# Two-operand GpSimd instructions of a hybrid decoder step: from whole tiles to pieces of at most 256 elements

## Chip, core and metric

The kernel runs on one core of a Trainium2 chip. The metric is the device time of one execution in microseconds (us); lower is better. Engines are named as the profile names them: PE (TensorE), DVE (VectorE), ACT (ScalarE), POOL (GpSimd), SP (SyncE, which issues the DMAs).

## The reference

One decoder layer over a prompt of 2048 tokens of 1024 features and 8 decoding sequences of 4 tokens, all in float32:

```python
h = rmsnorm(x, g_mix)
proj = h @ w_in                         # u | q | k | v | g
ssm_out = s5_mixer(u, ...)              # diagonal complex state space, scan over tokens, GELU, GLU
ret_out = retention_mixer(q, k, v, g)   # 4 heads, rope on q and k, chunks of 128, group norm, gate
x = x + concat([ssm_out, ret_out]) @ w_out
x = x + memory_attend(rmsnorm(x, g_xattn), mk, mv, w_mq, w_mo)   # 4 heads, 256 memory tokens
h = rmsnorm(x, g_mlp)
x = x + square(relu(h @ w_up)) @ w_down
y = rmsnorm(x, g_final)
```

The new states of the scan and the retention and the memory's keys and values are outputs too.

## The kernel before

Every matmul of float32 operands is made of three passes: an operand is split into a high part, rounded by ACT to the matmul's number format, and a low part, the operand minus its high part, by DVE or POOL. Activations lie with features in the partitions and tokens along the row, in four blocks of 512 tokens; the second block also carries the 32 sample tokens, so its tiles are 544 wide. Weights come in units of 128 x 1024 (`raw`), are split into `whl` and used at once.

The work has two large parts. The **mixer** (the first 990 us) goes through the four blocks: projection to v, then for each of four heads q, k and g (`head_items`), then u. Beside the projections run side chains: the retention of a head (`retention`: transposes `pkd`, products `psc`, `pkv`, `po`, a group norm on DVE, transpose `pt`), and the scan of the block before (`s5_batch`, four batches a block: matmuls `vr`, `vi`, DVE and POOL turn and scan them, matmul `py`, transpose `pf`). The memory's keys and values and the fold of the query and output weights follow, with the last block's scan beside them. The **rest** (990 us to the end) takes each block through attention (`sc`, softmax, `ptp`), the MLP (`up_items`, `down_items`) and the output projection of the next block.

The order on all engines is written at build time by a recording layer. `Engine.__getattr__` (line 189) wraps every call of an engine: it tells a planner (`Model.done`) what is written and read and then issues the instruction. The planner holds a time at which each engine comes free; it charges POOL 140 ns for an instruction and 2.11 ns an element, DVE 65 ns and 1.042 ns. PE's main stream of projections polls side chains whose planned wake time has come (`Order.poll`), so a planned duration sets after which matmul a chain's next matmul stands. Work with the key `E("...")` goes to DVE or POOL by a table (`SET`: 0 DVE, 1 POOL, 2 the one that the planner has done sooner); the weights' low part may be left open in the same way. Each engine then works through its own queue strictly in that order.

POOL makes: the low parts of some weight units, in four instructions of 256 elements each (`split_unit`, `lo`); and, in one instruction each, the second half of rope (`kr` and `qr`, 512 or 272 wide), four to six steps of each scan batch (`t`, `gl`, `Yi`; 512 or 4 x 129 = 516 elements), the sums of squares for the norms (`acc`), the low part of the MLP's activation (`actl`, 512 or 544), the tables of the scan at the start, and some smaller things. All calls go through line 197, so the trace has one line for them and is read by tile names.

Of the kernel before, what the change touches and what calls it, by code (L numbers as in the profile page):

```python
# [10 lines left out]
F32 = mybir.dt.float32  # L11
# [3 lines left out]
ALU = mybir.AluOpType  # L15
# [167 lines left out]
class Engine:  # L183
# [5 lines left out]
    def __getattr__(self, name):  # L189
        f = getattr(self.eng, name)  # L190

        def call(*args, **kw):
            outs = [x for x in ([kw["out"]] if "out" in kw else list(args[:1])) + [kw.get("accum_out")] if x is not None]
            ins = [x for x in list(args[0 if "out" in kw else 1:]) + [v for k, v in kw.items() if k not in ("out", "accum_out")]
                   if isinstance(x, bass.AP)]
            self.model.done(self.key, name, outs, ins, args[2] if name == "activation" else None)
            return f(*args, **kw)  # L197
        return call


class Either:
# [127 lines left out]
def tile_decoder_step(ctx: ExitStack, tc: tile.TileContext, ins: dict, outs: dict):  # L329
    nc = tc.nc  # L330
    model = Model()
    V, A, G, SY = (Engine(model, e, k) for e, k in ((nc.vector, "V"), (nc.scalar, "A"), (nc.gpsimd, "G"), (nc.sync, "SP")))
# [90 lines left out]
    def split_unit(raw, eng, pool=None, tag="whl", bufs=NW):  # L423

        hl = (pool or wpool).tile([P, 2, 1024], F32R, tag=tag, name=tag, bufs=bufs)
        A.activation(hl[:, 0, :], raw, AF.Copy)

        def lo():
            e = eng or min((V, G), key=lambda e: max(model.free[e.key], model.ready(hl)) + 1024 * Model.RATE[e.key][1])
            n = 256 if e is G else 1024  # L430
            for i in range(0, 1024, n):
                e.tensor_tensor(out=hl[:, 1, i:i + n], in0=raw[:, i:i + n], in1=hl[:, 0, i:i + n].bitcast(F32), op=ALU.subtract)
        return hl, lo

    od = Order(model, load_unit, split_unit)
# [46 lines left out]
    def pieces(t):  # L482
        return [(0, t)] if t <= 512 else [(0, t // 2), (t // 2, t // 2)]
# [1891 lines left out]
```

## Time and profile before

| What | Value |
|---|---|
| median of three runs | 3056.98 us (3055.93 to 3063.95) |
| profiled execution, device time | 3057.99 us |
| its span | 3055.8 us, 2.2 us less than its device time |
| PE busy | 2944.5 us, 96% of the span |
| DVE, ACT, POOL busy | 1767.3 us (58%), 1007.1 us (33%), 1314.5 us (43%) |
| instructions on POOL | 1463 |

The page's table of slices shows PE at eight or nine tenths in most slices of the first third and at nine tenths or more nearly everywhere later; DVE is at seven to nine tenths in the first quarter of the span and at three to five tenths later. A busy POOL or DVE instruction in the records includes the time in which it has begun and waits for a port.

### The profile page before, as it was taken

The page shows a single profiled execution, that of the slowest core. Times are in us where ns is not written, and L with a number is a line of the kernel's source. Part 1 is how long each engine was busy: PE and PEld are TensorE (multiplying, and loading weights), DVE is VectorE, ACT ScalarE, POOL GpSimd, SP SyncE. Part 2 cuts the span into 40 slices and gives each one's busy share as a digit, 9 for nine tenths or more (in the row PEclk, how much of TensorE's full clock was granted, in tenths as well). Part 3 has the DMA queues.
Part 4 walks back from the last instruction along what each step waited for, and adds up shares of the span by engine and source line. Part 5 has one row for each costly group of instructions (what it writes and reads, how often), then busy time and mean ns, then how long its engine had stood idle before and what let it go on. Part 6 is the DMA issues. An engine that isn't in the chain of part 4 may idle for free.

```text
span 3055.8 us, 43238 instructions
## 1 busy us (share of the span) xinstructions
PE 2944.5 (96%) x16676; PEld 2561.3 (84%) x16676; DVE 1767.3 (58%) x3088; ACT 1007.1 (33%) x1440; POOL 1314.5 (43%) x1463
## 2 busy tenths in 40 slices
PE   8898899998989999999999999999999999999998
PEld 6688788877987978888987888788999998978887
DVE  8968858779675654334465555556533444553334
ACT  4442232322454332223333333433322223432222
POOL 5534434344565153334534344462433326153334
PEclk9999999999999999999999999999999999999999
DMA  5453253342685222234324444542222233232222
GB/s 151 137 171 111 83 154 119 115 156 75 230 269 168 90 93 95 96 97 141 114 88 145 145 149 148 198 134 83 91 84 90 90 132 122 81 99 94 96 90 76
DMA packets 138957, 374.37 MB, mean 123 GB/s; under 512 B 18656, under 2 KB 39808, under 8 KB 138752
## 3 DMA queue, kind: packets, MB, share of 16 engines
q1 hardware_dynamic: 138176, 371.10, 37.3%
q8 instruction: 131, 2.15, 0.3%
q14 instruction: 74, 0.61, 0.1%
q10 hardware_dynamic: 576, 0.52, 0.1%
HBM read 334.17 MB, written 37.40 MB: 122 GB/s over the span
## 4 chain that ended last, share of the span: by engine, by line
PE 65%; DVE 1%; issue 0%; DMA 0%; ACT 0%; POOL 0%; POOLq 0%; SPq 0%; ACTq 0%; DVEq 0%
PE dn L447 57%; PE sc L447 6%; PE zps L447 1%; DVE rst L197 1%; PE ptp L451 0%; PE st L447 0%; DVE rsy L197 0%; DMA raw<-in_w_down 0%; DVE act L197 0%; PE sp L447 0%; POOL x L197 0%; DVE mx L197 0%; ACT x L197 0%; DVE stage L197 0%; DVE ms L197 0%
## 5 line engine op out<-in xcount | busy, mean ns | idle before, releaser
L447 PE MATMUL dn<-actl,whl 128*128 128x512 f32 (+2 forms) x4656 | 916.3, 356 | 2.2 <-DVE x L197 2.2
L447 PE MATMUL dn<-act,whl 128*128 128x512 f32 (+2 forms) x4704 | 913.3, 348 | 2.1 <-POOL whl L197 1.6
L197 POOL TENSOR_TENSOR whl<-raw,whl 128x256 fp32r<-128x256 f32 x896 | 692.7, 805 | 510.8 <-ACT whl L197 494.3
L447 PEld LDWEIGHTS dn<-actl,whl 128*128 128x128 f32 x4656 | 767.7, 188 | 130.5 <-ACT whl L197 1.9
L447 PEld LDWEIGHTS dn<-act,whl 128*128 128x128 f32 x4704 | 752.7, 189 | 110.8 <-issue 3.0
L197 ACT ACTIVATE whl<-raw 128x1024 fp32r<-128x1024 f32 (+1 forms) x505 | 523.2, 1046 | 650.7 <-PE dn L447 460.5
L197 DVE TENSOR_TENSOR x<-dn,x 128x512 f32<-128x512 f32 (+2 forms) x496 | 291.4, 606 | 430.7 <-PE dn L447 430.2
L197 DVE TENSOR_TENSOR whl<-raw,whl 128x1024 fp32r<-128x1024 f32 (+1 forms) x281 | 400.0, 1429 | 174.3 <-ACT whl L197 164.2
L447 PE MATMUL dn<-z,whl 128*128 128x512 f32 (+1 forms) x2160 | 435.1, 352 | 0.0
L447 PEld LDWEIGHTS dn<-z,whl 128*128 128x128 f32 x2160 | 353.4, 188 | 56.5 <-issue 1.1
L197 POOL TENSOR_TENSOR actl<-sq,actl 128x512 fp32r<-128x512 f32 (+1 forms) x128 | 171.2, 1338 | 455.0 <-DVE sq L197 445.4
L197 DVE SCALAR_TENSOR_TENSOR relu<-dn,rb 128x512 f32<-128x512 f32 (+1 forms) x160 | 91.6, 589 | 323.4 <-PE dn L447 316.0
L197 ACT ACTIVATE actl<-relu 128x512 fp32r<-128x512 f32 (+1 forms) x128 | 82.2, 642 | 512.5 <-DVE relu L197 512.5
L447 PE MATMUL dn<-whl,act 128*128 128x512 f32 x768 | 203.0, 413 | 11.6 <-ACT whl L197 6.3
L197 POOL TENSOR_TENSOR acc<-acc,relu 128x512 f32<-128x512 f32 (+2 forms) x77 | 107.4, 1394 | 237.1 <-ACT relu L197 235.0
L447 PEld LDWEIGHTS dn<-whl,act 128*128 128x128 f32 x768 | 168.0, 255 | 35.9 <-ACT whl L197 7.0
L197 DVE TENSOR_TENSOR sq<-relu 128x512 f32<-128x512 f32 (+1 forms) x128 | 91.6, 715 | 14.8 <-POOL actl L197 2.3
L447 PE MATMUL sc<-whl,act 128*128 128x256 f32 x576 | 80.3, 291 | 14.2 <-ACT p L197 9.4
L447 PEld LDWEIGHTS sc<-whl,act 128*128 128x128 f32 x576 | 75.1, 197 | 15.6 <-ACT p L197 10.0
L447 PE MATMUL sc<-whl,z 128*128 128x256 f32 x576 | 80.8, 291 | 0.0
L197 DVE SCALAR_TENSOR_TENSOR act<-x,small,act 128x512 fp32r<-128x512 f32 (+2 forms) x76 | 64.4, 854 | 28.2 <-ACT act L197 28.2
L197 ACT ACTIVATE act<-x,small 128x512 fp32r<-128x512 f32 (+2 forms) x76 | 53.0, 701 | 72.8 <-DVE x L197 52.9
(318 smaller groups left out, 2671.8 us busy)
## 6 DMA issues: line engine op xcount, KB each, us to landing
raw<-in_w_up SPq DMA_DIRECT2D x128, 512.0 KB, 3.5
raw<-in_w_down SPq DMA_DIRECT2D x128, 512.0 KB, 3.5
raw<-in_w_out SPq DMA_DIRECT2D x32, 512.0 KB, 3.5
raw<-wq_d SPq DMA_DIRECT2D x32, 512.0 KB, 3.5
raw<-wo_d SPq DMA_DIRECT2D x32, 512.0 KB, 3.5
x<-in_xT SPq DMA_DIRECT2D x48, 256.0 KB, 4.3
pm<-pm_d SPq DMA_DIRECT2D x16, 768.0 KB, 5.3
tab<-tab_d SPq DMA_DIRECT2D x16, 516.0 KB, 4.4
```

The source lines that it names most:

```text
L197: return f(*args, **kw)
L447: T.matmul(out, lhsT, rhs, start=start, stop=stop)
```

## The change

`Engine.__getattr__` looks at every `tensor_tensor` of POOL. If it has more than 256 elements a partition, the new `Engine.pieces` cuts it along its longest dimension into as many equal pieces as are needed for at most 256 elements, tells the planner of each, and issues each as an instruction of its own. 512 elements become 2 x 256; 544 become 182, 182 and 180; 272 become 2 x 136; 4 x 129 become three of 4 x 43; 4 x 128 become two of 4 x 64. `split_unit` loses its own loop, since POOL's share of a weight unit is cut by the new rule into the same four pieces. Instructions of other kinds, and those of DVE, keep their size.

```diff
@@ class Engine, call
+            n = int(np.prod(kw["out"].shape[1:])) if name == "tensor_tensor" else 0
+            if self.key == "G" and n > 256:
+                return self.pieces(f, kw)
             self.model.done(self.key, name, outs, ins, args[2] if name == "activation" else None)
             return f(*args, **kw)
         return call
+
+    def pieces(self, f, kw):
+
+        shape = kw["out"].shape
+        d = max(range(1, len(shape)), key=lambda i: shape[i])
+        rest = int(np.prod(shape[1:])) // shape[d]
+        parts = -(-shape[d] * rest // 256)
+        step = -(-shape[d] // parts)
+        for i in range(0, shape[d], step):
+            cut = (slice(None),) * d + (slice(i, min(i + step, shape[d])),)
+            part = {k: v[cut] if isinstance(v, bass.AP) else v for k, v in kw.items()}
+            self.model.done(self.key, "tensor_tensor", [part["out"]], [part["in0"], part["in1"]])
+            f(**part)
@@ split_unit, lo
-            n = 256 if e is G else 1024
-            for i in range(0, 1024, n):
-                e.tensor_tensor(out=hl[:, 1, i:i + n], in0=raw[:, i:i + n], in1=hl[:, 0, i:i + n].bitcast(F32), op=ALU.subtract)
+            e.tensor_tensor(out=hl[:, 1, :], in0=raw, in1=hl[:, 0, :].bitcast(F32), op=ALU.subtract)
```

POOL's program grows from 1468 to 1949 instructions, by 481. The other engines have the same work, but for a few instructions that the planner now gives to the other of DVE and POOL. Since the planner is told of the pieces, parts of the order move as well. The projections and products of the third mixer block, of the MLP stages and of the attention stand where they stood, but for single matmuls of the norms (`st`, `sp`); the matmuls of the side chains in the first two mixer blocks, in the last one and of the last two scan batches move.

The first place is on POOL, in the third mixer block, at the fourth scan batch and the fourth head (`t_5111` and `t_5242` are the same tile of that batch under the two programs' numbers). Before:

```order
L197 TENSOR_TENSOR whl<-raw,whl 128x256 x4
L197 TENSOR_TENSOR gl<-Yi,tab 128x516
L197 TENSOR_TENSOR Yi<-Yi,tab 128x516
L197 TENSOR_TENSOR t_5111<-t_5111,Yi 128x516
L197 COPY carr<-t_5110 128x4
L197 COPY cari<-t_5111 128x4
L197 TENSOR_TENSOR qr<-qr,tmp 128x512
L197 TENSOR_TENSOR kr<-kr,tmp 128x512
```

After, in the same place:

```order
L214 TENSOR_TENSOR whl<-raw,whl 128x256 x4
L214 TENSOR_TENSOR gl<-Yi,tab 128x4x43 x3
L214 TENSOR_TENSOR Yi<-Yi,tab 128x4x43 x3
L214 TENSOR_TENSOR t_5242<-t_5242,Yi 128x4x43 x3
L200 COPY carr<-t_5241 128x4
L200 COPY cari<-t_5242 128x4
L214 TENSOR_TENSOR qr<-qr,tmp 128x256 x2
L214 TENSOR_TENSOR kr<-kr,tmp 128x256 x2
```

Nothing moved there; only the sizes differ.

The second place is on PE, in the last mixer block, from the transpose `pu` of the block's second scan batch to the product `py` of the first. Before:

```order
L447 MATMUL dn<-whl,act 128x512 x12
L451 MATMUL pu<-ident,tm_5731 128x128 x4
L447 MATMUL dn<-whl,act 128x512 x18
L447 MATMUL py<-pm_5778,u_5785 128x128
L447 MATMUL py<-pm_5778,t_5925 128x128
```

After:

```order
L461 MATMUL dn<-whl,act 128x512 x12
L465 MATMUL pu<-ident,tm_5872 128x128 x4
L461 MATMUL dn<-whl,act 128x512 x36
L461 MATMUL py<-pm_5919,u_5926 128x128
L461 MATMUL py<-pm_5919,t_6070 128x128
```

36 instead of 18 projection matmuls stand between them. Of the four `pkd` of this block, the first two stand 6 and 9 such matmuls later, the third and fourth 9 and 3 earlier.

The third place is on POOL, at the start of the second block's attention: the last sums of squares `acc`, copies for the sample, and two weight units. Before:

```order
L197 COPY xs<-x 128x32
L197 TENSOR_TENSOR acc<-acc,relu 128x544 x3
L197 CAST pmk<-act 128x64 x2
L197 TENSOR_TENSOR whl<-raw,whl 128x256 x8
L197 CAST pmk<-act 128x64 x2
```

After:

```order
L200 COPY xs<-x 128x32
L214 TENSOR_TENSOR acc<-acc,relu 128x182 x2
L214 TENSOR_TENSOR acc<-acc,relu 128x180
L214 TENSOR_TENSOR acc<-acc,relu 128x182 x2
L214 TENSOR_TENSOR acc<-acc,relu 128x180
L214 TENSOR_TENSOR acc<-acc,relu 128x182 x2
L214 TENSOR_TENSOR acc<-acc,relu 128x180
L200 CAST pmk<-act 128x64 x2
L214 TENSOR_TENSOR whl<-raw,whl 128x256 x8
L200 CAST pmk<-act 128x64 x2
```

Three instructions of 544 elements have become nine in front of the weight units; on PE the matmuls `st` that read `acc` stand six products `sc` of 256 columns later, here and in the other three blocks.

## Rows read from the trace of the kernel before

**Rows 1.** The page: each engine's busy time, share of the span and instructions.
```profile
PE 2944.5 (96%) x16676; PEld 2561.3 (84%) x16676; DVE 1767.3 (58%) x3088; ACT 1007.1 (33%) x1440; POOL 1314.5 (43%) x1463
```
**Rows 2.** Busy time by stretch: length, PE, PEld, DVE, ACT, POOL, granted clock, DMA.
```profile
0.00:400.00 400.00, 353.90 (x2025) 305.29 (x2026) 326.87 (x784) 139.47 (x204) 197.79 (x230) 0.96 0.44 135
400.00:990.00 590.00, 552.72 (x3227) 482.91 (x3226) 432.51 (x777) 215.26 (x328) 279.13 (x273) 0.99 0.49 158
1092.00:1490.00 398.00, 398.00 (x1917) 333.73 (x1916) 167.32 (x213) 110.07 (x135) 167.81 (x197) 1.00 0.33 111
```
**Rows 3.** Waits of PE: who waited for whom, us in total, times, longest.
```profile
PE pt L451 <- DVE scs L197: 13.9, 7, 4.4
PE py L447 <- DVE t L197: 12.2, 9, 3.2
PE pkd L451 <- POOL kr L197: 11.4, 10, 2.1
PE sc L447 <- ACT p L197: 9.7, 4, 3.5
...
PE sc L447 <- DVE act L197: 4.7, 2, 4.3
PE dn L447 <- POOL whl L197: 4.4, 6, 0.9
...
PE pn L447 <- POOL rsc L197: 3.1, 2, 2.1
...
PE po L447 <- DVE s L197: 2.0, 1, 2.0
```
**Rows 4.** Timeline, second block's attention: POOL weight pieces beside small DVE steps (start, us).
```profile
1495.81 5.55 POOL L197 TENSOR_TENSOR whl<-raw,whl 128x256 fp32r<-128x256 f32 x8
1500.06 0.65 DVE L197 TENSOR_TENSOR rst<-rsy 128x5 f32<-128x5 f32 x1
1501.42 0.17 DVE L197 SCALAR_TENSOR_TENSOR rst<-rst 128x5 f32<-128x5 f32 x1
```
**Rows 5.** Timeline, POOL in an MLP stage, alone at its port.
```profile
1257.26 1.29 POOL L197 TENSOR_TENSOR actl<-sq,actl 128x512 fp32r<-128x512 f32 x1 [4.22 <-DVE sq L197]
1258.51 2.84 POOL L197 TENSOR_TENSOR whl<-raw,whl 128x256 fp32r<-128x256 f32 x4
```
**Rows 6.** Timeline, end of the mixer and, last, the same DVE step elsewhere.
```profile
980.54 7.01 POOL L197 TENSOR_TENSOR acc<-acc,x 128x512 f32<-128x512 f32 x4
984.71 4.05 DVE L197 SCALAR_TENSOR_TENSOR act<-x,small,act 128x512 fp32r<-128x512 f32 x3
986.47 1.31 PE L447 MATMUL sc<-whl,act 128*128 128x256 f32 x6 [4.32 <-DVE act L197]
...
2045.52 1.41 DVE L197 SCALAR_TENSOR_TENSOR act<-x,small,act 128x512 fp32r<-128x512 f32 x2
```
**Rows 7.** Timeline, third block's fourth scan batch: DVE, POOL and the waiting PE.
```profile
541.25 2.30 DVE L197 TENSOR_TENSOR t<-Yr,tab 128x516 f32<-128x516 f32 x2
543.70 2.13 POOL L197 TENSOR_TENSOR t<-t,Yi 128x516 f32<-128x516 f32 x1 [0.69 <-DVE t L197]
544.61 1.76 DVE L197 SCALAR_TENSOR_TENSOR gate<-gth,gate 128x512 f32<-128x512 f32 x1
547.57 0.66 DVE L197 TENSOR_TENSOR t<-t,gl 128x516 f32<-128x516 f32 x1
548.29 0.71 PE L447 MATMUL py<-pm,t 128*128 128x128 f32 x4 [3.17 <-DVE t L197]
```
**Rows 8.** Timeline, last mixer block: `py` waits while POOL is idle; a `kr` beside DVE.
```profile
633.31 1.23 DVE L197 TENSOR_TENSOR whl<-raw,whl 128x1024 fp32r<-128x1024 f32 x1 [4.17 <-ACT whl L197]
635.20 1.19 PE L447 MATMUL py<-pm,t 128*128 128x128 f32 x3 [3.22 <-DVE t L197]
723.57 1.49 POOL L197 TENSOR_TENSOR kr<-kr,tmp 128x512 f32<-128x512 f32 x1 [4.03 <-DVE tmp L197]
```
**Rows 9.** PE in the MLP of the first block, 12 matmuls of 512 columns in a row.
```profile
1252.65 2.94 PE L447 MATMUL dn<-z,whl 128*128 128x512 f32 x12
```

## The prediction

> **What bounds the kernel now.** I read the page's head first: PE is busy 2944.5 of 3055.8 us, so no more than 111 us can come from anything but faster matmuls [rows 1]. The table of stretches tells where these lie [rows 2]. In the mixer PE is busy 353.9 of the first 400 us and 552.7 of the next 590: it idles 46.1 and 37.3 us, 83.4 together. In an MLP stage (1092 to 1490 us) it is busy in all of the 398 us, although POOL works in 168 of them. So what POOL's cut does in the MLP costs or gives nothing, and the mixer decides. There DVE is busy 82 and 73% of the time, POOL 49 and 47%. The granted clock is 0.96 and 0.99 of full in the two stretches, which says that some of the time PE ran at 1.2 instead of 2.4 GHz, and more so where it idled more; the missing shares, 0.04 x 400 + 0.01 x 590, are 22 us beside 83.4 us of idleness, 0.26 us for each idle us. I let every us of idleness count 1.26 us.
>
> The waits of PE by name [rows 3] say on whom: eight rows of the mixer name a DVE step (`pt` 13.9, `py` 12.2, six more from 4.7 down to 2.0; 47.6 us together), `pkd` waits 11.4 us for POOL's `kr`, weights and `rsc` of POOL cost 4.4 and 3.1, and 9.7 us go to the softmax at the start of attention.
>
> The view that ties DVE to POOL is the timeline of two of them together. A DVE step of five elements takes 0.17 us once POOL's eight weight pieces are over and 0.65 us while they run [rows 4]: a DVE instruction with two operands in SBUF doesn't proceed while a POOL instruction of this kind holds what they share, and it waits for the end of that one instruction.
>
> **Part 1, length of a hold.** Alone, POOL takes 1.29 us for 512 elements and 2.84 / 4 = 0.71 us for 256 [rows 5]. So a cut 512 takes 1.42 us, 0.13 us more; the slope is (1.29 - 0.71) / 256 = 2.27 ns an element, which makes 172 elements 0.13 + 0.39 = 0.52 us and 544 elements in three pieces 1.6 us instead of some 1.36. The 481 further instructions are 63 us of POOL time, estimated; in the MLP the idle half of POOL hides them, and if that cover were gone they would cost at most their share on the path, which the rows give no sign of.
>
> What DVE gains is read at three waits. At 548.3 us `py` waited 3.17 us for `t<-t,gl` [rows 7]; in the queue ahead of it two DVE steps took 2.30 us where one of the same size takes 0.66, and `gate` took 1.76, with POOL's 516-element steps between them: 1.0 and 1.1 us lost to two holds. With holds of 0.52 us the loss is at most 1.0, a gain of 1.1 us, 35% of the wait. At 986.5 us [rows 6] three `act` steps took 4.05 us where two take 1.41 elsewhere, so 1.9 us were lost beside POOL's four `acc`; a hold of 0.71 instead of 1.29 returns 45% of it, 0.9 of 4.32 us. At 635.2 us [rows 8] `py` waited 3.22 us because DVE's weight step ahead had waited 4.17 us for ACT: nothing to gain. Together 2.0 of 10.7 us, 19%; of 47.6 us that is **-9 us**. The lower end is 0, where DVE meets the second piece with its next instruction and pays twice; the upper one 35%, -17.
>
> **Part 2, the order.** Of the matmuls that moved, two places weigh. In the last mixer block 18 more projection matmuls of 2.94 / 12 = 0.245 us [rows 9] stand ahead of the `py` that waited 3.22 us [rows 8]; 4.4 us of work cover it if the data come as before: -3.2. The `pkd` of that block stand 6 and 9 matmuls later, 9 and 3 earlier. The first three wait some 2 us now (2.1 is the longest [rows 3]): -1.5 and -2 against +2.2 and +0.7, -0.6. In the first two blocks the retention stands 3 to 15 matmuls later, which adds cover for `pt` and `po`, but DVE is nearly full there and much of it is in part 1; I add -1. Sum **-5 us**, between -10 and +3.
>
> **Part 3, who waits for POOL.** Each `kr` of 512 becomes 0.13 us longer at best. If DVE takes a turn between the halves, a turn of 0.66 us as in rows 7 comes on top. `kr` took 1.49 us with almost no disturbance [rows 8]. Ten waits: +1.3 to +8; I take 0.3 each, **+3 us**, near the low end, since several of the DVE steps behind it read PSUM. Eight waits for POOL's weights and `rsc`, each with a cut instruction or two in the queue ahead: 0.13 to 0.26 each, **+1 us** (0 to 2). At the start of attention the last `acc` of 544 are three pieces each, some 0.2 us longer, and `st` stands six matmuls of half width, 0.7 us, later, in front of a chain of small DVE steps that ends three softmax waits of 3 us: **+2 us** (0 to 4).
>
> **Sum.** -9 - 5 + 3 + 1 + 2 = -8 us idle, times 1.26 is -10.1. The profiled execution took 3058.0 us (span 3055.8 and 2.2 around it), which makes 3047.9; it lay 1 us above the median of 3057.0, and what is measured is a median, so **3047 us**. The rivals are put on the median in the same way.
>
> **The rivals.** Nothing comes of it: DVE pays at both pieces, and PE finds another late step where one was repaired. Part 1 is then -3, part 2 -3, the rest +6, and the time 3057. For it speaks that DVE's runs are long, so that its next instruction is ready at once; against it that in rows 7 `gate` is followed by steps that read PSUM and need no turn.
>
> Slower: POOL starves. Each cut is one more place where DVE can come in between. Where a DVE instruction with two operands in SBUF is ready at more than half of the cuts, a `kr` takes 0.71 + 0.66 + 0.71 = 2.1 instead of 1.49 us. Part 3 becomes +7, +2 and +4, part 1 is 0 because `py` then waits for POOL's half of the scan, and part 2 at -3 leaves +10, times 1.26 is +12.6: 3070 us. For it: four `acc` already take 7.01 instead of 4 x 1.29 = 5.16 us beside DVE's `act` [rows 6], and they would have four more gaps. Against it: POOL's other chains have slack, as at 548 us, where its last step ended 2.5 us before `py` started [rows 7]. The Trainium skill (SBUF — State Buffer, "Who interferes with whom") states this as a lock that the one who issues first holds for the whole instruction while the other is blocked fully; by that rule the cut moves time from POOL to DVE rather than saving it, and the time would be that of this rival wherever POOL is the later one. The trace agrees on the block (0.65 against 0.17 us, rows 4); whom it favours after a cut no row shows.
>
> Much faster: all DVE waits behave as the one of rows 7. Part 1 is -17, the sum -16, times 1.26 is -20.2: 3037 us. It needs POOL's large instructions to be in every run of DVE that PE waits for, and rows 8 show one that has none.
>
> **How the numbers follow.** A measurement of this kernel can tell some 0.3%, 9 us, from no change: faster is below 3047.8, slower above 3066.2. The forecast, with a spread of 3040 to 3053, has 0.38; nothing 0.24; starving 0.21; much faster 0.17. Faster is 0.17 and two thirds of 0.38: 0.42. Slower is the larger part of starving and a tail of nothing: 0.20. Same is the rest, 0.38. The bounds of the terms added up reach from -33 to +22 us, which is too wide for terms that do not all go one way; the range is 3034 to 3067, which leaves out about a tenth on each side.
>
> **What would show it.** In the profile after: single DVE steps behind POOL wait 0.7 us at most, and `t<-Yr` and `gate` become shorter; the 512-element group of `actl` is gone for 256 at about 0.72 us; `py` and `pt` lose some 10 us of PE's waits, `pkd` gains 1 to 5; PE in the MLP stays full. I'm wrong on part 1 if DVE's busy time in the mixer stays within 10 us of before; wrong on part 3 if `pkd` waits over 18 us; wrong on the cover if PE idles in the MLP.

## The result, and the profile after

The changed kernel takes 3084.03 us (median of four runs, 3082.26 to 3085.98) against 3057.34 before: 1.0083 times as long, 95% interval 1.0066 to 1.0101. The change costs some 25 us where a gain of 10 was forecast, and lies above the range.

The page's first part and the mean granted clock, of before and then of after (the page's line of before is in [rows 1]):

```profile
core 0: 3055.8 us, clock 0.988
```
```profile
PE 2962.4 (96%) x16676; PEld 2569.2 (83%) x16676; DVE 1748.5 (57%) x3085; ACT 1006.7 (33%) x1440; POOL 1452.0 (47%) x1944
...
core 0: 3080.4 us, clock 0.985
```

The span grew by 24.6 us. PE's idle time, the span less PE's busy time, went from 111.3 to 118.0 us: only 6.7 us. PE is *busy* 17.9 us longer with the same 16676 matmuls. The share of the clock that was not granted went from 0.012 to 0.015 of the span, from some 37 to some 46 us: 9 or 10 of the 17.9. The other eight are not the clock: 3.3 of them lie in one stretch of the MLP (last section), and where the rest lies was not found.

A stretch between two fixed times no longer holds the same work after the change, since everything behind the mixer comes 17 us later. So this is the whole mixer, up to the first `sc` of attention, before and after:

```profile
0.00:979.30 979.30, 900.71 (x5217) 782.99 (x5218) 750.02 (x1554) 350.66 (x524) 468.91 (x499) 0.98 0.47 149
```
```profile
0.00:996.20 996.20, 913.91 (x5217) 791.87 (x5218) 741.03 (x1552) 350.25 (x524) 530.03 (x715) 0.97 0.46 146
```

PE makes the same 5217 matmuls in 16.9 us more, 13.2 of them busy. DVE is 9.0 us less busy in the mixer, and as much again behind it (18.8 in all). PE's waits, as in [rows 3]:

```profile
PE sc L461 <- ACT p L200: 12.4, 4, 4.0
PE pt L465 <- DVE scs L200: 10.8, 7, 3.5
PE py L461 <- DVE t L200: 9.9, 8, 2.5
PE dn L461 <- POOL whl L214: 9.9, 9, 3.7
PE pkd L465 <- POOL kr L214: 7.3, 15, 1.1
...
PE st L461 <- DVE acc L200: 5.6, 3, 3.2
```

`pt`, `py` and `pkd` lost 3.1, 2.3 and 4.1 us. Waits for weights of POOL (+5.5) and for `acc` (from 1.1 to 5.6) came in their place, where the order has moved. Which of these differences the pieces made and which the order, the experiments tell.

### The profile page after: what moved, and what is told of

Its sections match the earlier page's. It is cut to its first block, busy times and chain, and to the rows that moved or that the text cites. A ratio compares the mean times of both kernels' runs of the same rounds, so it can differ in the third digit from the quotient of the medians.

```text
span 3080.4 us, 43757 instructions
## 1 busy us (share of the span) xinstructions
PE 2962.4 (96%) x16676; PEld 2569.2 (83%) x16676; DVE 1748.5 (57%) x3085; ACT 1006.7 (33%) x1440; POOL 1452.0 (47%) x1944
## 4 chain that ended last, share of the span: by engine, by line
PE 62%; DVE 2%; POOL 1%; issue 1%; ACT 1%; DMA 0%; POOLq 0%; SPq 0%; ACTq 0%; DVEq 0%
PE dn L461 54%; PE sc L461 6%; PE zps L461 1%; POOL acc L214 1%; DVE rst L200 1%; PE ptp L465 0%; DVE x L200 0%; POOL whl L214 0%; PE st L461 0%; DVE rsy L200 0%; DVE act L200 0%; ACT relu L200 0%; DMA raw<-in_w_down 0%; ACT act L200 0%; PE sp L461 0%
## 5 line engine op out<-in xcount | busy, mean ns | idle before, releaser
L214 POOL TENSOR_TENSOR actl<-sq,actl 128x256 fp32r<-128x256 f32 (+2 forms) x288 | 219.7, 786 | 418.3 <-DVE sq L200 407.8
L214 POOL TENSOR_TENSOR acc<-acc,relu 128x256 f32<-128x256 f32 (+1 forms) x161 | 129.3, 832 | 217.7 <-ACT relu L200 212.0
L461 PEld LDWEIGHTS sc<-whl,z 128*128 128x128 f32 x576 | 75.1, 196 | 3.0 <-POOL whl L214 3.0
```

What stands on the lines that cost most here:

```text
L214: f(**part)
L461: T.matmul(out, lhsT, rhs, start=start, stop=stop)
```

## Experiments

Two theories stood after the result. *Holds*: POOL loses the port at the new cuts, and what waits for it is late. *Order*: the planner, told of pieces, has put side chains in worse places. Fourteen kernels tell them apart. The first two have small edits of their own to the effect that the table gives. The others are made by one edit with two switches, by the block in which the planner stands (0 to 3 the mixer blocks, the memory's weights with the last; 4 the rest). The names of the runs count the blocks from 1:

```diff
+            told = cut = self.key == "G" and n > 256
+            told, cut = told and self.model.phase in TOLD, cut and self.model.phase in CUT
+            if not told:
                 self.model.done(self.key, name, outs, ins, ...)
+            if not told and not cut:
+                return f(*args, **kw)
+            for part in self.pieces(kw):
+                if told:
+                    self.model.done(self.key, name, [part["out"]], [part["in0"], part["in1"]])
+                if cut:
+                    f(**part)
+            if not cut:
+                f(**kw)
```

TOLD are the blocks in which the planner is told of pieces, CUT those in which pieces are issued; before has neither, after has both everywhere. With TOLD empty and the planner's costs as they were, PE, DVE and ACT have the order of before, instruction for instruction. The two pool_cost runs have no pieces, but another cost in the plan and so another order. The weights' four pieces of 256 stay in all of them. Ratios are to the kernel before on the same chip; its median lay between 3054.4 and 3058.2 us, so medians of different rows are not compared with each other. rope_only and scan_only choose what is cut by the step instead of the block.

| Run | TOLD | CUT | median, us | ratio (95%) |
|---|---|---|---|---|
| the change | all | all | 3084.0 | 1.0083 (1.0066 to 1.0101) |
| pieces_old_order | none | all | 3059.0 | 1.0006 (0.9994 to 1.0017) |
| new_order_whole | all | none | 3074.0 | 1.0062 (1.0049 to 1.0074) |
| told_blocks_1_2 | 0, 1 | none | 3068.3 | 1.0041 (1.0024 to 1.0058) |
| told_block_1 | 0 | none | 3061.1 | 1.0023 (1.0011 to 1.0034) |
| told_block_2 | 1 | none | 3062.9 | 1.0027 (1.0016 to 1.0038) |
| told_rest | 2, 3, 4 | none | 3060.1 | 1.0014 (1.0001 to 1.0026) |
| pool_cost_160 | none | none | 3070.0 | 1.0044 (1.0026 to 1.0061) |
| pool_cost_120 | none | none | 3066.9 | 1.0038 (1.0026 to 1.0050) |
| pieces_block_4 | none | 3 | 3046.1 | 0.9964 (0.9947 to 0.9981) |
| pieces_blocks_1_4 | none | 0, 3 | 3047.9 | 0.9973 (0.9957 to 0.9989) |
| pieces_blocks_2_3 | none | 1, 2 | 3062.9 | 1.0014 (1.0003 to 1.0026) |
| pieces_rest | none | 4 | 3055.7 | 1.0006 (0.9995 to 1.0017) |
| rope_only | none | `kr`, `qr` | 3056.4 | 0.9998 (0.9984 to 1.0013) |
| scan_only | none | scan steps | 3055.5 | 0.9994 (0.9980 to 1.0008) |

### The pieces or the order

> POOL's large two-operand instructions are issued in pieces as in the changed kernel, but the planner is told of the whole instruction, so that PE, DVE, ACT and SP have the order of the kernel before, instruction for instruction. Hold theory (POOL loses the shared port at the new cuts, and what waits for POOL comes later): most of the 27 us of loss is here, 3075 to 3085 us. Order theory (the planner, told of more expensive pieces, has moved the side chains to worse places): 3050 to 3060 us, since with the old order only the shorter holds are left, and the DVE waits py and pt shrink from 12.2 and 13.9 us.

> The order of the changed kernel on PE, DVE, ACT and SP, instruction for instruction, but POOL's large instructions are issued whole, except the weights' low parts, which stay at 256 elements as before. Hold theory: the loss goes away, 3053 to 3062 us. Order theory: most of the loss stays, 3075 to 3085 us, with the idle time and the 1.2 GHz stretches of PE in the first 480 us as in the changed kernel (53 us idle there against 48 before).

The order theory holds. The pieces alone cost 0.06%, no more than can be told from nothing; the order alone, with POOL's instructions as long as before, costs 0.62%, 19 us (15 to 23). Together 0.68%, inside the interval of the change. One part of the expectation failed: `pt` did not shrink (below). PE's line on the page, of the pieces in the old order and then of the new order with whole instructions:

```profile
PE 2948.8 (97%) x16676; PEld 2563.2 (84%) x16676; DVE 1748.5 (57%) x3088; ACT 1006.2 (33%) x1440; POOL 1435.9 (47%) x1932
```
```profile
PE 2956.6 (96%) x16676; PEld 2567.4 (84%) x16676; DVE 1775.3 (58%) x3085; ACT 1006.3 (33%) x1440; POOL 1325.4 (43%) x1466
```

In the first, DVE has the 1748.5 us of the changed kernel, 19 less than before: that saving belongs to the pieces. In the second PE is busy 12.1 us longer than before although no instruction has changed in length, and idle 4.3 us more. Most of the 12.1 is clock again (granted 0.985 as after the change, 9 or 10 us), and 3.3 is the stretch of the MLP.

PE's waits for the three tiles that fell after the change, with the pieces in the old order and then in the new order with whole instructions:

```profile
PE pt L466 <- DVE scs L200: 13.9, 7, 4.5
PE py L462 <- DVE t L200: 10.6, 8, 2.4
PE pkd L466 <- POOL kr L213: 10.5, 15, 1.2
```
```profile
PE py L464 <- DVE t L200: 12.2, 8, 3.5
...
PE pt L468 <- DVE scs L200: 9.0, 6, 3.2
...
PE pkd L468 <- POOL kr L217: 7.2, 8, 1.4
```

Before they were 13.9, 12.2 and 11.4 us. So `py` fell by the pieces; `pt` and most of `pkd` fell by the new order, which makes these waits shorter and others longer.

### Where the order costs

> Order only: every POOL instruction is issued at its old size. The planner is told of pieces while the first two mixer blocks are planned, and of whole instructions after that; on PE only matmuls of the first two blocks move. If the order's loss of 17 us lies in the first two blocks, where the trace of the new order with whole instructions is 10 us behind by 430 us: 3066 to 3072 us. If it lies at the end of the mixer and in attention: 3053 to 3060 us.

> Order only, the complement: the planner is told of whole instructions in the first two mixer blocks and of pieces from the third block to the end. First theory: 3055 to 3064 us, since the trace of the new order lies behind by no more than 7 us after 430 us. If the late moves cost it (the weights of the memory waiting for POOL at 912 us, st six products later in attention): 3066 to 3073 us. The two halves should add up to some 17 us.

> Order only, instructions at their old size; the planner is told of pieces while the first mixer block is planned. In the trace of both blocks PE is 4 us ahead at 180 us and 5 us behind at 400 us. If the second block's moves alone cost: 3052 to 3058 us here. If any shift costs: 3061 to 3068 us.

> Order only; the planner is told of pieces while the second mixer block is planned (matmuls between 180 and 400 us move). If the loss of 13 us of both blocks lies here: 3066 to 3072 us. If the two blocks share it: 3060 to 3065 us.

The loss is no single place. The two halves cost 0.41 and 0.14%, the first and the second block alone 0.23 and 0.27%: my guess that the first block gains by its moves is refuted, and the parts add up to the whole within their intervals. In the stretch of the second block (from the 480th projection matmul to the 1248th), busy times of before, then of the new order with whole instructions, then of the changed kernel:

```profile
182.40:396.10 213.70, 191.22 (x1271) 170.55 (x1270) 164.61 (x393) 57.38 (x85) 101.92 (x122) 0.98 0.38 119
```
```profile
178.90:404.60 225.70, 197.09 (x1269) 175.10 (x1267) 167.12 (x393) 58.52 (x88) 101.24 (x123) 0.95 0.38 120
```
```profile
183.60:409.10 225.50, 197.98 (x1269) 175.13 (x1267) 162.31 (x393) 58.34 (x89) 112.76 (x173) 0.95 0.39 119
```

The same work takes 12 us longer with or without pieces. PE's idle time in it grew from 22.5 to 28.6 us, and the missing clock from 0.02 x 214 = 4 to 0.05 x 226 = 11 us.

One of the new waits can be read to its cause. The norm of the second block's activations ends with `act` on ACT, `act` and `acc` on DVE, then `st` on PE. ACT's queue before, and then ACT, DVE and PE after:

```profile
183.93 0.74 ACT L197 ACTIVATE act<-x,small 128x544 fp32r<-128x544 f32 x1
...
185.12 0.74 ACT L197 ACTIVATE act<-x,small 128x544 fp32r<-128x544 f32 x1
...
186.31 0.58 ACT L197 ACTIVATE u<-pu 128x512 f32<-128x512 f32 x1
```
```profile
184.56 1.74 ACT L200 ACTIVATE tm<-km 32x512 f32<-32x512 f32 x4 [3.90 <-DVE km L200]
188.97 0.60 ACT L200 ACTIVATE u<-pu 128x512 f32<-128x512 f32 x1 [2.67 <-DMA pm_d<-tm]
...
190.41 0.74 ACT L200 ACTIVATE act<-x,small 128x544 fp32r<-128x544 f32 x1
...
191.18 0.79 DVE L200 SCALAR_TENSOR_TENSOR act<-x,small,act 128x544 fp32r<-128x544 f32 x1 [6.71 <-ACT act L200]
...
193.99 1.21 PE L461 MATMUL st<-ones,acc 128*128 128x2 f32 x10 [3.16 <-DVE acc L200]
```

Before, the two `act` stood ahead of `u<-pu`, and four `tm<-km` stood one pair of `act` earlier. After, `tm<-km` and `u<-pu` stand ahead of the two `act`, and ACT waited 3.90 us for DVE and 2.67 us for a DMA before them. ACT worked off its queue in order, so DVE idled 6.71 us for `act` (1.33 before), and PE 3.16 us for `acc`, for which it did not wait before. Nothing here has to do with the length of a POOL instruction: in the new order with whole instructions ACT waits 3.58 and 2.68 us at the same place. In the last block it is POOL's own queue: the weights that PE needs now stand behind two steps of a scan batch.

```profile
911.41 2.22 POOL L214 TENSOR_TENSOR gl<-Yi,tab 128x172 f32<-128x172 f32 x3
...
913.60 2.91 POOL L214 TENSOR_TENSOR Yi<-Yi,tab 128x172 f32<-128x172 f32 x3
916.47 4.21 POOL L214 TENSOR_TENSOR whl<-raw,whl 128x256 fp32r<-128x256 f32 x4
...
917.24 1.01 PE L461 MATMUL dn<-kt,whl 128*128 128x256 f32 x3 [3.70 <-POOL whl L214]
```

That is the largest part of the 5.5 us by which PE's waits for POOL's weights grew. With whole instructions in the same order PE waits 2.56 us here, so the order makes most of it and the pieces add 1.1.

### Is it the pieces' order, or any other order?

```diff
-    RATE = {"V": (65.0, 1.042), "A": (80.0, 0.834), "G": (140.0, 2.11)}
+    RATE = {"V": (65.0, 1.042), "A": (80.0, 0.834), "G": (160.0, 2.11)}
```

> No pieces at all, neither issued nor told; the planner charges 160 instead of 140 ns for a POOL instruction. This moves matmuls of the side chains in the first two mixer blocks, in the last one and after it, as the change does, for a reason that has nothing to do with pieces. If the loss is specific to the order that pieces give (their own chains waiting longer): 3050 to 3062 us. If the table of offsets fits the old order alone, so that any shift of the planned times costs: 3063 to 3085 us.

> No pieces; the planner charges 120 instead of 140 ns for a POOL instruction, the opposite of the run with 160. If the table fits the old order alone and any shift costs: 3063 to 3075 us. If dearer POOL instructions in the plan are what costs: 3045 to 3058 us.

Both shifts cost: 0.44% with 160 ns, 0.38% with 120, with no piece anywhere. The plan's cost of a POOL instruction may go up or down; all seven runs with another plan, for all of the kernel or a part, are slower than the old one. So the table of offsets and engine choices seems to fit the sequence that the old costs produce, and the other sequences tried from the same table lose 0.1 to 0.6%. A table chosen anew for the planner that knows of pieces wasn't tried; how fast that would be is open.

### What the pieces do, where the order is kept

> The old order, and POOL's large instructions cut only in the last mixer block with the memory's weights behind it (590 to 990 us); everything else whole. In the trace of pieces with the old order this stretch runs 9 us shorter than before, and the stretches ahead of it 5 us longer. If the cut shortens holds where PE waits for DVE: 3046 to 3052 us. If those 9 us are noise of single executions: 3054 to 3060 us.

> The old order; cut only in the first and the last mixer block with the memory's weights. If the first block gains by its own as the trace of all pieces shows (2.5 us by 182 us): 3043 to 3047 us, the fastest so far. If the first block is even or loses: 3047 to 3053 us.

> The old order; cut only in the second and third mixer block. All pieces in the old order cost nothing while the pieces of the last block alone gained 8 to 11 us, so the rest of the pieces must lose some 10 us. If they lose it here, where with all pieces this stretch ran 5 to 8 us longer: 3061 to 3068 us. If each stretch gains or is even, and the sum was noise: 3050 to 3057 us.

> The old order; cut only behind the mixer (attention, MLP, output projection), where the prediction set the cut at +2 us at the start of attention and at nothing in the MLP. If that cover holds: 3057 to 3062 us. If the parts add up (all pieces +2, blocks 2 and 3 +4, blocks 1 and 4 -8 us): +6, 3061 to 3066 us, with the matmuls of the MLP 0.2 to 0.5% slower, as in the traces of all pieces.

The pieces gain 0.36% (0.19 to 0.53) in the last mixer block and the memory's weights, which is 11 us by this ratio and 8 by the medians (3046.1 to 3054.5 on that chip). They lose 0.14% in the second and third block, and do nothing that can be told behind the mixer (3055.7 us, below both ranges that were expected); the first block adds no gain of its own. pieces_block_4 is faster than both kernels.

`kr` and `pkd` in the last block's second head, before and with the pieces:

```profile
691.74 1.49 POOL L197 TENSOR_TENSOR kr<-kr,tmp 128x512 f32<-128x512 f32 x1 [5.53 <-DVE tmp L197]
...
693.29 1.09 PE L451 MATMUL pkd<-ident,kr 128*128 128x128 f32 x4 [2.06 <-POOL kr L197]
```
```profile
687.09 1.52 POOL L208 TENSOR_TENSOR kr<-kr,tmp 128x256 f32<-128x256 f32 x2 [4.39 <-DVE tmp L203]
...
687.86 0.44 PE L474 MATMUL pkd<-ident,kr 128*128 128x128 f32 x2 [0.73 <-POOL kr L208]
...
688.66 0.44 PE L474 MATMUL pkd<-ident,kr 128*128 128x128 f32 x2 [0.36 <-POOL kr L208]
```

Each transpose reads 128 columns of `kr`. The first two start after the first piece and run while POOL makes the second: 0.73 + 0.36 us in place of 2.06. This is the best of the four heads; together they wait 6.1 us with whole instructions and 4.8 to 5.0 with pieces. The wait at the mixer's end fell as well (before: 4.32 us behind three `act` of 4.05 us [rows 6]):

```profile
974.91 2.30 DVE L203 SCALAR_TENSOR_TENSOR act<-x,small,act 128x512 fp32r<-128x512 f32 x2
...
976.13 1.22 PE L470 MATMUL sc<-whl,act 128*128 128x256 f32 x4 [2.51 <-DVE act L203]
```

A third place is among the memory's weights: PE waits for DVE's `wst`, which stands in DVE's queue behind two `t<-Yr` that run beside scan steps of POOL. Before, and then with the scan steps alone cut:

```profile
889.01 3.39 DVE L197 TENSOR_TENSOR t<-Yr,tab 128x516 f32<-128x516 f32 x2
...
894.39 2.21 PE L447 MATMUL dn<-whl,vt 128*128 128x512 f32 x5 [3.33 <-DVE wst L197]
```
```profile
887.24 2.74 DVE L203 TENSOR_TENSOR t<-Yr,tab 128x516 f32<-128x516 f32 x2
...
891.29 1.66 PE L473 MATMUL dn<-whl,vt 128*128 128x512 f32 x6 [0.36 <-DVE wst L203]
```

Counted from the same matmul of PE, DVE reaches the `t<-Yr` 1.6 us earlier with the cut steps, and gets from there to `wst` in 3.6 instead of 4.9 us.

In the second and third block the other side of the cut can be read. The second scan batch of the third block, before and with all pieces in the old order:

```profile
474.05 1.68 POOL L197 TENSOR_TENSOR Yi<-Yi,tab 128x516 f32<-128x516 f32 x1
...
479.19 0.68 DVE L197 TENSOR_TENSOR t<-t,gl 128x516 f32<-128x516 f32 x1
...
479.93 0.71 PE L447 MATMUL py<-pm,t 128*128 128x128 f32 x4 [1.41 <-DVE t L197]
```
```profile
478.39 3.39 POOL L213 TENSOR_TENSOR Yi<-Yi,tab 128x172 f32<-128x172 f32 x3
...
481.73 2.03 POOL L213 TENSOR_TENSOR t<-t,Yi 128x172 f32<-128x172 f32 x3
...
483.28 1.04 DVE L200 TENSOR_TENSOR t<-t,gl 128x516 f32<-128x516 f32 x1
484.38 0.71 PE L462 MATMUL py<-pm,t 128*128 128x128 f32 x4 [1.70 <-DVE t L200]
```

The three pieces of `Yi` take 3.39 instead of 1.68 us: DVE's `t<-Yr` and its weights, with two operands in SBUF, run in the same time and come in between:

```profile
478.14 1.78 DVE L200 TENSOR_TENSOR t<-Yr,tab 128x516 f32<-128x516 f32 x2
...
479.84 1.54 DVE L200 TENSOR_TENSOR whl<-raw,whl 128x1024 fp32r<-128x1024 f32 x1
```

POOL's next step starts later and now stands beside DVE's last one, which takes 1.04 instead of 0.68 us, and `py` waits 0.3 us longer. The wait is 1.68 to 1.70 us in the three traces in old order with these scan steps cut, and 1.39 to 1.42 in the other five. The Trainium skill (SBUF — State Buffer, "Who interferes with whom") says that whoever issues first holds the shared ports for its whole instruction; these rows agree, and show what it means for a cut: each piece has to win the ports again. How much of the 0.14% comes from such places isn't shown. From 182 to 581 us of before, the same PE work takes 406 us in the two traces with all pieces of these blocks and 398 to 401 in the four with none, but PE idles only 1 to 5 us more; the rest is matmuls that took longer, in part at a lower clock (0.97 and 0.98, against 0.99 in before).

> The old order; of POOL's instructions only the second half of rope, kr and qr, is cut, in all four mixer blocks. Release theory: the transposes pkd read kr in columns of 128, so two of the four start after the first piece; a wait of 2.05 us becomes 0.73 + 0.36, and of the 11.4 us that pkd waits for kr some 5 to 7 go: 3046 to 3052 us. The prediction's step (a cut kr is later by 0.13 us and a turn of DVE, +3 us): 3057 to 3062 us.

> The old order; only POOL's steps of the scan batches are cut (516 into three pieces, 512 into two). Hold theory, the prediction's part 1: DVE is held less, py waits less than 12.2 us, 3048 to 3055 us. If DVE pays again at the next piece (t<-t,gl took 1.04 instead of 0.68 us with all pieces in the old order): 3055 to 3062 us.

Neither group of instructions by itself moves the time: -0.02% and -0.06%, both within 0.2% of nothing; the first time lies in neither of its ranges, the second between them. With the rope alone cut, `pkd` waited 11.0 us in 17 waits of at most 1.1 us, against 11.4 in 10 of at most 2.1: it fell by 1.5 us in the last block and grew by as much in the others.

Which cut gains in the last block can be read from the traces, since PE has the same matmuls in the same order in all eight kernels with the old order. PE's idle time ahead of the same matmul (named by its start in before), in us:

| Place in the last block | whole there (before, pieces_blocks_2_3, pieces_rest) | rope_only | scan_only | all cut there (pieces_old_order, pieces_block_4, pieces_blocks_1_4) |
|---|---|---|---|---|
| `sc` at 986.5, end of the mixer | 4.32, 4.30, 4.32 | 4.32 | 4.32 | 2.50, 2.51, 2.50 |
| `dn` at 894.4, for `wst` | 3.33, 1.89, 3.29 | 2.02 | 0.36 | 0.10, 1.29, 0.10 |
| `po` at 736.2 | 1.37, 1.40, 1.40 | 1.40 | 0.38 | 0.35, 0.35, 0.35 |
| `py` at 741.8 | 1.19, 1.19, 1.19 | 0.65 | 1.19 | 0.65, 0.65, 0.65 |
| `pkd`, four heads | 6.2, 6.1, 6.1 | 4.6 | 5.8 | 4.9, 4.8, 5.0 |
| all idle time, 581 to 990 | 30.6, 27.7, 27.7 | 28.0 | 25.0 | 22.3, 24.4, 23.3 |
| length of this stretch | 409.0, 406.3, 405.2 | 405.7 | 402.5 | 399.0, 399.2, 398.3 |

The stretch is some 8 us shorter with all cuts, which is the gain of pieces_block_4. About half of it comes with the scan steps alone and about 1 us with the rope. The rest needs another cut; nearly 2 us of it lie at the `sc`, which neither scan nor rope moves and in front of which the cut `acc` stand. Single executions differ by up to 4 us in this stretch, so the shares are rough. The `sc` and `dn` are waits for a DVE that POOL's instructions hold, as part 1 of the prediction has it.

## Why the prediction was wrong

**Part 2, the order, is the step that failed.** It was -5 us of idle time, between -10 and +3, or -6 us of time; measured alone it is +19 us of time, with 4.3 us more idle in the trace. I priced the order by two places at which cover grew and by PE's matmul count ahead of waits that I knew. These two places gained as forecast or more: the `py` that waited 3.22 us at 635 us doesn't wait at all after the change, and `pkd` lost 4.2 us by the order alone, where 0.6 was forecast. But the `py` of the fourth batch of that block waits 2.52 us where it waited 1.19 (3.47 with whole instructions). What I left out is that a moved side chain carries its instructions on ACT, DVE and POOL with it, and that these queues are worked off in order: `u<-pu` ahead of `act` and scan steps ahead of the weights made new waits of 3.16 and 3.70 us. A bound of +3 for some 80 moved places in an order whose planner and table belong together was far too narrow; in the two runs with another POOL cost a shift of the plan cost +12 and +13.

**The clock factor, 1.26, was mis-sized too.** With the new order alone PE idled 4.3 us more (111.3 to 115.6) and lost 9 or 10 us more of clock. With the pieces alone it idled 6.8 us less (104.5) and the time didn't fall, since PE was busy 4.3 us longer. There is no fixed price for an idle us here, as the last section shows.

**Part 1, the holds, was right in its mechanism and not in its worth.** At the `py` of [rows 7] the two `t<-Yr` went from 2.30 to 1.79 us, `gate` from 1.76 to 1.01, and the wait from 3.17 to 2.37: 0.8 us, of 1.1 forecast. It is 2.36 or 2.37 in every trace with these scan steps cut, and 3.16 or 3.17 in every other one. At the `sc` of [rows 6] 4.32 became 2.36 us; 0.9 was forecast and 2.0 came. At the `py` of [rows 8] I expected nothing, and no effect can be told: two traces with whole instructions in that block have 1.30 and 1.81 us in place of 3.22, three with pieces 2.21 to 2.74.

Summed over the same eight rows as in the prediction, DVE's waits fell from 47.6 to 39.2 us with the pieces alone: 8.4, of 9 forecast. But `pt`, the largest, stayed at 13.9. DVE was 9.0 us less busy in the mixer, when I had called anything within 10 a sign against this part. And the pieces alone, all terms but part 2, were to bring (-9 + 3 + 1 + 2) x 1.26 = -4 us; they measure +2 (-2 to +5), because the second and third block lose what the last one gains.

The lower end, that DVE and POOL meet again at every piece, came true too, in the second and third block.

**Part 3 had one sign wrong, by little.** With the pieces alone `pkd` was to wait 3 us more; it waited 0.9 us less (0.4 with the rope alone). I had `kr` finished as a whole, while its readers want a part of it. That it waits 4.1 us less after the change is the order's doing. The start of attention was +2 and measures +2.7 (9.7 to 12.4 us), with +0.7 by the pieces alone and +0.9 by the order alone. The cover in the MLP held within what can be told: pieces_rest is +0.06% (-0.05 to +0.17).

**The rivals.** "Starves" gave 3070 us, nearest to the truth by its number, which was luck: with the old order POOL's pieces cost nothing in sum. None of the rivals was a worse order, and that is why the range missed.

## What to carry to other kernels

Where a planner's costs decide the order, an edit that the planner sees is two changes: the instructions, and a new order everywhere behind the first difference. Time them apart, by issuing the new instructions under the old plan, before judging either, and then block by block. Here nothing was gained by all pieces under either plan, while the pieces of one block under the old plan gained 8 to 11 us. Cutting an instruction can pay where its reader needs only a part, or where a neighbour on the same port is the later one; where both engines are busy at that port, each cut is one more place to lose it.

## What the runs showed of the hardware

The granted clock doesn't follow from a wait. The last `py` of the third block waits 3.17 us in before and 3.17 us in told_blocks_1_2, where the block's PE work stands in the same order. The 18 us from just ahead of each `py`, busy times of before and then of told_blocks_1_2:

```profile
548.00:566.00 18.00, 17.71 (x114) 14.90 (x115) 12.16 (x34) 4.25 (x7) 2.09 (x4) 1.00 0.30 103
```
```profile
553.40:571.40 18.00, 17.70 (x87) 15.20 (x88) 8.54 (x28) 3.59 (x6) 1.59 (x3) 0.63 0.21 74
```

In one the clock stayed at 2.4 GHz; in the other the mean is 0.63, so most of the 18 us ran at 1.2 GHz, and 87 matmuls instead of 114 were done. Twelve of the 16 traces have this wait, of 3.16 or 3.17 us, with the full clock in the 20 us ahead of the wait: behind it the mean is 1.00 in seven, 0.91 in three and 0.63 or 0.64 in two. What decides it is not in these rows. before, pieces_rest and pieces_block_4 run the same instructions up to there and have 1.00, 1.00 and 0.91, so single executions of the same work can differ.

The MLP of the first block runs at one of two rates. In 250 us at full clock, with PE never idle, before and after made:

```profile
1180.00:1430.00 250.00, 250.00 (x1090) 204.13 (x1090) 102.35 (x121) 64.97 (x77) 95.61 (x115) 1.00 0.34 111
```
```profile
1180.00:1430.00 250.00, 250.00 (x1079) 202.28 (x1078) 104.61 (x120) 63.68 (x76) 96.29 (x135) 1.00 0.33 109
```

From one matmul to the same later one (those at 1180.06 and 1430.22 us in before) it is 250.16 us in seven of the 16 traces and 252.83 in nine, 1% more, and nothing between. Over 1092 to 1490 us of before it is 3.3 us: that much of the eight that PE was busy longer off the clock's account after the change. The slow rate stands in kernels with and without pieces. Seven of the eight kernels with another order have it, the changed one among them, and two of the eight with the old order. Its cause wasn't found. Whether it belongs to a kernel or changes from one execution to the next was not looked at; if it belongs to the kernel, up to 3 of the order's 19 us are this rate and no wait.
